# First half of the SSD output projection: ten of its eleven late units as five pairs by seven products of quarters, the residual kept in DRAM, weight buffers of half the size

## The chip, the cores and the metric

The kernel runs on one core of a Trainium2 chip. The metric is device time in microseconds (us) of one execution. Engines are named as in the profile: PE (TensorE, matmuls), PEld (its weight loads), DVE (VectorE), ACT (ScalarE), POOL (GpSimd) and SP (SyncE, which issues most DMAs).

## The reference

Two layers over 512 tokens of width 2048: a Mamba-2 SSD mixer, then a stick-breaking attention mixer; each is followed by a gate from the residual. The change lies in the first layer's output projection, `y @ out_w` with K = 4096, and in its residual.

```python
def reference(x, p, norm_w, ssd_in_w, ...):
    h = x
    for i in range(DEPTH):
        u = rms_norm(h, norm_w[i])
        if i % N_MIXERS == 0:
            mix = ssd_branch(u, ...)      # ends in  y @ out_w,  y (512, 4096), out_w (4096, 2048)
        else:
            mix = sb_branch(u, ...)       # ends in  o @ out_w,  o (512, 2048)
        h = h + mix
        gate = sigmoid(rms_norm(h, ple_norm_w[i]) @ ple_gate_w[i])
        h = h + (p[i] @ ple_proj_w[i]) * gate
    return h
```

## The kernel before

Everything is laid out transposed: a tile has 128 features (partitions) by T = 512 tokens. An fp32 operand is split into a high and a low part, `ah`, `al` for activations and `wh`, `wl` for weights, and each product is three matmuls (h x h, h x l, l x h). The high part is a cast on ACT, the low part a subtraction on DVE (`split`, L144/L145; `block`, L135 load, L137 cast, L139 subtraction).

A `unit` makes one output tile of 128 features: K/128 k-tiles, three matmuls of 512 columns each, in one PSUM bank (`mmp`, tag "mm", four banks). A `pair` makes two output tiles at once, and for 8 of its 16 k-tiles it may use the seven-product scheme (Strassen, in Winograd's form) on 2 x 2 quarters: two output tiles by two k-tiles for the weights, two k-tiles by two halves of 256 tokens for the activations. The sums of weight quarters come from `wforms` (S1 to S4, one call per four k-tiles, b = 0 and 1), the sums of activation halves from `xforms` (`th`, `tl`, from a raw tile U and a scratch US; SP = 4 of them cover 8 k-tiles). Its seven products go to four banks Z, W, X, Y, each product three matmuls of 256 columns for g = 0 and g = 1, so 84 matmuls for both b; the other eight k-tiles are `plain`, 24 matmuls of 512 for each of the two output tiles. Afterwards ACT and DVE combine the banks (L279 to L283, then L291 for each output tile) in a tile E, and `emit` takes the result. With `late` the plain products come first.

The output projection of the SSD layer has K = 4096, 32 k-tiles of `y`, which stands in DRAM (`y_d`). Its first half, k-tiles 0 to 15, is done by 16 units: five (j < EARLY) at the end of the scan, with the residual x added and the sum written to `h_d` (L666 to L671), and eleven afterwards (L777 to L779), added to `h[j]` in SBUF; the 16 tiles `h[j]` are loaded by SP (L774). The second half is eight pairs with `forms` (L781 to L784), whose eight k-tiles are 16 to 23; `staged2` loads its 16 k-tiles as eight tiles U through POOL's queue (two buffers, L707) and splits them. Each pair's `emit` is `add_h` (L722).

The attention layer's output projection (`w_sp`, `w_sq`) uses the same `pair` and `wforms`; there several pairs have no plain products. PE's instructions run in program order. The other engines' orders come from a scheduler; what stands in `high_priority` (the weights, in `block` and `wforms`) is put ahead of the rest. Each engine works its queue in order, and a DMA queue's issues wait in order too.

## Time and profile before

| what | value |
|---|---|
| median of 3 runs | 2732.29 us (2732.17 to 2732.33) |
| the profiled execution's own time | 2730.93 us |
| its span | 2729.0 us |
| PE busy | 2718.0 us, 13242 matmuls |
| DVE, ACT, POOL busy | 1654.1, 1299.9, 379.9 us |
| DMA | 304.81 MB, mean 112 GB/s |

The span runs from the first to the last instruction of the profiled execution; its own time is 1.93 us more. An engine's busy time is what its instructions took; idle time of an engine that nobody waits for costs nothing. PE's waits say where the others came late.

### The profile page before, as it was taken

What the parts mean: (1) busy time and instruction counts of PE and PEld (TensorE: products, weight loads), DVE (VectorE), ACT (ScalarE), POOL (GpSimd) and SP (SyncE); (2) the same over time, 40 slices, a digit from 0 to 9 for tenths busy, and PEclk for the clock granted to TensorE, in tenths of its full rate; (3) what the DMA queues carried; (4) which work ended last, traced back from release to release, by engine and by line L of the source; (5) the groups of instructions that cost most, each with busy time, mean ns of one, the idle gap of its engine ahead of it and who ended that gap; (6) DMA issues with size and microseconds to landing.
All of it is one profiled execution on the core that took longest, in us unless ns stands there. A gap on an engine that the chain in (4) does not pass through costs nothing.

```text
span 2729.0 us, 34056 instructions
## 1 busy us (share of the span) xinstructions
PE 2718.0 (100%) x13242; PEld 2267.4 (83%) x13242; DVE 1654.1 (61%) x2203; ACT 1299.9 (48%) x2014; POOL 379.9 (14%) x406
## 2 busy tenths in 40 slices
PE   9999999999999999999999999999999999999999
PEld 7888888888888888889888888888888888889887
DVE  8665566565565675376744547647647647779533
ACT  6554545546464553243432436646546546544321
POOL 2222121222222121011110100000000000112000
PEclk9999999999999999999999999999999999999999
DMA  4343323334243447243333322322222222343342
GB/s 170 114 128 99 124 93 124 101 116 128 94 135 94 142 143 247 93 143 105 101 101 94 100 93 93 93 89 87 88 97 85 87 91 88 106 158 105 112 124 85
DMA packets 110257, 304.81 MB, mean 112 GB/s; under 512 B 11472, under 2 KB 27472, under 8 KB 110096
## 3 DMA queue, kind: packets, MB, share of 16 engines
q1 hardware_dynamic: 106576, 291.10, 33.7%
q0 software_dynamic: 3520, 11.54, 1.3%
q8 instruction: 104, 1.70, 0.3%
q14 instruction: 57, 0.47, 0.1%
HBM read 284.37 MB, written 18.22 MB: 111 GB/s over the span
## 4 chain that ended last, share of the span: by engine, by line
PE 95%; DVE 2%; DMA 1%; ACT 1%; issue 1%; POOL 0%; SPq 0%; DVEq 0%; POOLq 0%; ACTq 0%
PE mm L57 79%; PE pv L57 6%; PE px_p L57 2%; PE px_r L57 1%; PE px_y L57 1%; PE px_z L57 1%; PE px_av L57 1%; PE px_o L57 1%; PE px_st L57 1%; PE px_qn L57 1%; PE px_x L60 1%; DMA raw<-in_w_op 0%; DVE al L145 0%; PE psB L57 0%; PE psd L57 0%
## 5 line engine op out<-in xcount | busy, mean ns | idle before, releaser
L57 PE MATMUL mm<-ah,wh 128*128 128x512 f32 (+1 forms) x3252 | 1257.9, 387 | 0.6 <-ACT ah L144 0.6
L57 PE MATMUL mm<-ah,wl 128*128 128x512 f32 (+1 forms) x3252 | 1249.5, 384 | 0.1
L57 PE MATMUL mm<-al,wh 128*128 128x512 f32 (+1 forms) x3252 | 1247.3, 384 | 1.5 <-DVE al L145 1.5
L139 DVE TENSOR_TENSOR wl<-raw,wh 128x1024 fp32r<-128x1024 f32 x424 | 529.7, 1249 | 413.3 <-ACT wh L137 412.2
L137 ACT CAST wh<-raw 128x1024 fp32r<-128x1024 f32 x424 | 444.6, 1049 | 646.7 <-PE mm L57 528.0
L57 PEld LDWEIGHTS mm<-ah,wl 128*128 128x128 f32 x3252 | 611.1, 188 | 123.4 <-DVE wl L139 0.4
L57 PEld LDWEIGHTS mm<-al,wh 128*128 128x128 f32 x3252 | 611.7, 188 | 121.1 <-DVE al L145 3.1
L57 PEld LDWEIGHTS mm<-ah,wh 128*128 128x128 f32 x3252 | 611.5, 188 | 116.9 <-issue 0.9
L685 POOL TENSOR_TENSOR ssq<-ssq,sq 128x512 f32<-128x512 f32 x45 | 68.0, 1512 | 407.3 <-ACT sq L684 407.3
L879 POOL TENSOR_SCALAR_AFFINE_SELECT lm<-lm 128x128 f32<-128x128 f32 x64 | 27.8, 434 | 614.9 <-DVE lm L878 612.1
L520 DVE SCALAR_TENSOR_TENSOR cv<-xr,vec,cv 128x512 f32<-128x512 f32 x144 | 109.7, 762 | 2.8
L57 PE MATMUL pv<-wh,ah 128*128 128x512 f32 x256 | 101.0, 395 | 0.0
L57 PE MATMUL pv<-wl,ah 128*128 128x512 f32 x256 | 99.9, 390 | 0.0
L57 PE MATMUL pv<-wh,al 128*128 128x512 f32 x256 | 99.7, 389 | 0.0
L592 ACT ACTIVATE M<-ab,act__458 128x128 f32<-128x128 f32 x256 | 84.0, 390 | 30.3 <-PE px_y L57 29.9
L210 ACT CAST wh<-raw 128x768 fp32r<-128x768 f32 (+1 forms) x60 | 54.6, 941 | 80.5 <-DVE raw L204 49.2
L313 ACT ACTIVATE sg<-cv 128x512 f32<-128x512 f32 x48 | 30.3, 632 | 125.7 <-DVE cv L520 125.6
L756 DVE TENSOR_TENSOR gt<-mm,rbc 128x512 f32<-128x512 f32 x32 | 22.1, 691 | 101.9 <-PE mm L57 101.8
L315 POOL TENSOR_TENSOR xc<-cv,sg 128x512 f32<-128x512 f32 x32 | 42.2, 1318 | 254.9 <-ACT sg L314 234.9
L876 DVE SCALAR_TENSOR_TENSOR lb<-px_z,e 128x128 f32<-128x128 f32 (+1 forms) x64 | 31.4, 490 | 72.6 <-ACT e L874 72.1
L211 DVE TENSOR_TENSOR wl<-raw,wh 128x768 fp32r<-128x768 f32 (+1 forms) x60 | 65.5, 1094 | 8.9 <-ACT wh L210 8.9
L57 PE MATMUL mm<-th,wh 128*128 128x256 f32 x240 | 68.0, 283 | 0.7 <-DVE h L779 0.7
(252 smaller groups left out, 3126.1 us busy)
## 6 DMA issues: line engine op xcount, KB each, us to landing
raw<-in_w_in SPq DMA_DIRECT2D x158, 512.0 KB, 3.5
raw<-in_w_sb SPq DMA_DIRECT2D x96, 512.0 KB, 3.5
raw<-in_w_gate SPq DMA_DIRECT2D x64, 512.0 KB, 3.9
ab<-ac_d SPq DMA_DIRECT2D x64, 256.0 KB, 3.4
raw<-in_w_oe SPq DMA_DIRECT2D x32, 512.0 KB, 3.6
raw<-in_w_op SPq DMA_DIRECT2D x32, 512.0 KB, 4.1
raw<-in_w_v SPq DMA_DIRECT2D x32, 512.0 KB, 3.6
y_d<-zs SPq DMA_DIRECT2D x32, 256.0 KB, 3.8
```

Source lines behind the costliest of these rows:

```text
L57: self._queue(self.tc.nc.tensor.matmul(out, lhsT, rhs, start=start, stop=stop, **kw), rows / 2370.0)
L137: S.copy(wh, raw)
L139: V.tensor_tensor(wl, raw, wh.bitcast(F32), op=ALU.subtract)
L210: S.copy(wh, raw)
L211: V.tensor_tensor(wl, raw, wh.bitcast(F32), op=ALU.subtract)
L313: S.activation(tmp, half, AF.Tanh)
L315: G.tensor_tensor(dst, half, tmp, op=ALU.mult)
L520: V.scalar_tensor_tensor(cv, xr[:, tap : tap + T], cw[:, u, tap : tap + 1], cv, op0=ALU.mult, op1=ALU.add)
L592: S.activation(M[:, c, :], ab[:, c * P : (c + 1) * P], AF.Relu, bias=act_[:, c, h : h + 1], scale=-1.0)
L685: G.tensor_tensor(ssq, ssq, sq, op=ALU.add)
L876: V.scalar_tensor_tensor(lb, pz, 0.0, e, op0=ALU.min, op1=ALU.subtract)
L879: G.affine_select(out=lm[:, :P], in_=lm[:, :P], compare_op=ALU.is_gt, fill=0.0, base=0, pattern=[[1, P]], channel_multiplier=-1,)
```

## The change

The unit j = 5 stays a unit; the ten units j = 6 to 15 become five pairs with seven products for k-tiles 0 to 7 (`first`: four forms, kept in the slots h0 to h7 of the residual's pool) and plain products for k-tiles 8 to 15; the first pair is `late`. The residual of these tiles no longer stands in SBUF: `set_down` loads x into one buffer hx, adds, and writes the sum to `h_d`, all DMAs on POOL's queue, and after the last pair 16 loads on POOL's queue bring the residual back as eight tiles hp. The second half's forms are made from the middle of the pairs on (j = 10). In `wforms` the quarters are loaded as they are, in 8 k-tiles of 128 columns, three of them split directly (768 columns), and S3, S1, S2, S4 made by four DVE operations of 256 columns in a tile Q of one buffer, then split (1024 columns). In `pair` the order of the seven products is A11, A12, A22, S3, S1, S2, S4 instead of A11, S3, S1, S2, A12, S4, A22, and E shares the tag and the two buffers of U. The raw weights have four buffers of 8 tiles (512 KB) instead of two of 16. The line numbers move by one or so: L697 to L707 becomes L706 for the U loads, L291 becomes L290, L281/L282/L283 become L280/L281/L282.

```diff
@@ -131,7 +131,7 @@
 
     def block(src, offset=4000):
         with tc.high_priority(offset=offset):
-            raw = wp.tile([P, 16, P], F32, tag="raw", name="raw", bufs=2)[:, :8, :]
+            raw = wp.tile([P, 8, P], F32, tag="raw", name="raw", bufs=4)
             nc.sync.dma_start(raw, src)
             wh = wp.tile([P, 8, P], F32R, tag="wh", name="wh")
             S.copy(wh, raw)
@@ -190,36 +190,35 @@
 
 
 
-
         with tc.high_priority(offset=4000):
-            F = wp.tile([P, 8, 2, P], F32, tag="raw", name="raw", bufs=2)
-            nc.sync.dma_start(F.rearrange("p (a b) g m -> p a b (g m)", b=2)[:, :, 0, :], src)
-            V.tensor_tensor(F[:, 1], F[:, 0], F[:, 2], op=ALU.subtract)
-            V.tensor_tensor(
-                F[:, 2:6].rearrange("p (a b) g m -> p a b (g m)", b=2)[:, :, 1, :],
-                F[:, 4].rearrange("p g m -> p (g m)").unsqueeze(1).broadcast_to([P, 2, 2 * P]),
-                F[:, 0:2].rearrange("p a g m -> p a (g m)"),
-                op=ALU.add,
-            )
-            V.tensor_tensor(F[:, 7], F[:, 6], F[:, 5], op=ALU.subtract)
-            out = []
-            for tag, a, b, pool in (("", 1, 5, wp), ("3", 5, 8, wq)):
-                wh = pool.tile([P, 2 * (b - a), P], F32R, tag="wh" + tag, name="wh")
-                wl = pool.tile([P, 2 * (b - a), P], F32R, tag="wl" + tag, name="wl")
-                raw = F[:, a:b].rearrange("p a g m -> p (a g) m")
-                S.copy(wh, raw)
-                V.tensor_tensor(wl, raw, wh.bitcast(F32), op=ALU.subtract)
-                out += [(wh, wl, 2 * i) for i in range(b - a)]
-        return out
-
-    def xforms(raw, i):
+            R = wp.tile([P, 8, P], F32, tag="raw", name="raw", bufs=4)
+            nc.sync.dma_start(R, src)
+            A21, A11, A22, A12 = (R[:, 2 * i : 2 * i + 2, :] for i in range(4))
+            Q = wq.tile([P, 8, P], F32, tag="Q", name="Q", bufs=1)
+            S3, S1, S2, S4 = (Q[:, 2 * i : 2 * i + 2, :] for i in range(4))
+            wh = wq.tile([P, 6, P], F32R, tag="wh3", name="wh")
+            wl = wq.tile([P, 6, P], F32R, tag="wl3", name="wl")
+            S.copy(wh, R[:, 2:8, :])
+            V.tensor_tensor(S3, A21, A11, op=ALU.subtract)
+            V.tensor_tensor(S1, A22, A21, op=ALU.add)
+            V.tensor_tensor(S2, A22, S3, op=ALU.add)
+            V.tensor_tensor(S4, A12, S2, op=ALU.subtract)
+            V.tensor_tensor(wl, R[:, 2:8, :], wh.bitcast(F32), op=ALU.subtract)
+            vh = wp.tile([P, 8, P], F32R, tag="wh", name="wh")
+            vl = wp.tile([P, 8, P], F32R, tag="wl", name="wl")
+            S.copy(vh, Q)
+            V.tensor_tensor(vl, Q, vh.bitcast(F32), op=ALU.subtract)
+        return [(wh, wl, 2 * i) for i in range(3)] + [(vh, vl, 2 * i) for i in range(4)]
+
+    def xforms(raw, i, slots=None):
 
         t = tp.tile([P, 4, H], F32, tag="US", name="US")
         V.tensor_tensor(t[:, 0:2], raw[:, 0:1].broadcast_to([P, 2, H]), raw[:, 1:3], op=ALU.subtract)
         V.tensor_tensor(t[:, 2], raw[:, 2], t[:, 0], op=ALU.subtract)
         V.tensor_tensor(t[:, 3], raw[:, 3], t[:, 2], op=ALU.subtract)
-        th = tp.tile([P, 4, H], F32R, tag=f"th{i}", name=f"th{i}")
-        tl = tp.tile([P, 4, H], F32R, tag=f"tl{i}", name=f"tl{i}")
+        pool, tags = slots or (tp, (f"th{i}", f"tl{i}"))
+        th = pool.tile([P, 4, H], F32R, tag=tags[0], name=f"th{i}")
+        tl = pool.tile([P, 4, H], F32R, tag=tags[1], name=f"tl{i}")
         split(th, tl, t)
         return th, tl
 
@@ -257,7 +256,7 @@
             plain(0, X)
             plain(1, Y)
         for b in range(len(forms) // 2):
-            S3, A11, S1, A22, S2, A12, S4 = wforms(src[:, b, :].rearrange("p (a n) -> p a n", a=4))
+            A11, A22, A12, S3, S1, S2, S4 = wforms(src[:, b, :].rearrange("p (a b) -> p a b", b=P))
             for m in range(7):
                 for g in range(2):
                     i = 2 * b + g
@@ -266,16 +265,16 @@
                     lo, hi = slice(0, H), slice(H, T)
                     seven(*(
                         (Z, 1, A11, g, ah[:, hi], al[:, hi]),
+                        (X, 1, A12, g, bh[:, hi], bl[:, hi]),
+                        (Y, 1, A22, g, th[:, 3], tl[:, 3]),
                         (W, 1, S3, g, th[:, 1], tl[:, 1]),
                         (W, 0, S1, g, th[:, 0], tl[:, 0]),
                         (Z, 0, S2, g, th[:, 2], tl[:, 2]),
-                        (X, 1, A12, g, bh[:, hi], bl[:, hi]),
                         (X, 0, S4, g, bh[:, lo], bl[:, lo]),
-                        (Y, 1, A22, g, th[:, 3], tl[:, 3]),
                     )[m])
                 fl.poll()
         if forms:
-            E = tp.tile([P, 4, H], F32, tag="E", name="E")
+            E = tp.tile([P, 4, H], F32, tag="U", name="E", bufs=2)
             S.copy(E[:, 1], Z[:, 1])
             U2 = tp.tile([P, T], F32, tag="gt", name="U2")[:, :H]
             V.tensor_tensor(U2, Z[:, 0], E[:, 1], op=ALU.add)
@@ -769,14 +768,31 @@
         wq = st.enter_context(tc.tile_pool(name="wq0", bufs=2, reuse_waits="tile"))
         tp = st.enter_context(tc.tile_pool(name="tp0", bufs=1, reuse_waits="tile"))
         lq = st.enter_context(tc.tile_pool(name="lq0", bufs=1, reuse_waits="tile"))
-        for j in range(KT):
-            h.append(lp.tile([P, T], F32, tag=f"h{j}", name=f"h{j}"))
-            nc.sync.dma_start(h[j], (h_d if j < EARLY else xT)[j * P : (j + 1) * P, :])
+
+        def set_down(j0):
+            def emit(o, e):
+                js = slice((j0 + o) * P, (j0 + o + 1) * P)
+                hx = lq.tile([P, T], F32, tag="sq2", name="hx")
+                G.dma_start(hx, xT[js, :])
+                V.tensor_tensor(hx, e, hx, op=ALU.add)
+                G.dma_start(h_d[js, :], hx)
+            return emit
+
+
+        first = [
+            xforms(quarters(from_dram(y_d), 2 * i), i, (lp, (f"h{2 * i}", f"h{2 * i + 1}"))) for i in range(SP)
+        ]
+        set_down(EARLY)(0, unit(w_oe[EARLY], acts))
+        for j in range(EARLY + 1, KT, 2):
+            if j == EARLY + 5:
+                forms = forms_of(from_dram(y_d), KT)
+            pair(w_of[(j - EARLY) // 2], acts, first, 0, set_down(j), late=j == EARLY + 1)
         ssq = rp.tile([P, T], F32, tag="ssq", name="ssq")
-        forms = forms_of(from_dram(y_d), KT)
-        for j in range(EARLY, KT):
-            ps = unit(w_oe[j], acts)
-            V.tensor_tensor(h[j], ps, h[j], op=ALU.add)
+        for j in range(0, KT, 2):
+            hp = lp.tile([P, 2, T], F32, tag=f"h{j // 2}", name="hp")
+            for q in range(2):
+                h.append(hp[:, q, :])
+                G.dma_start(h[j + q], h_d[(j + q) * P : (j + q + 1) * P, :])
         acts = staged2(y_d, KT, 2 * KT)
         for j in range(0, KT, 2):
             if j == KT - 2:
```

The weights of j = 6 to 15 are laid out as pairs on the host (`w_of`), and `h_d` has all 16 tiles.

**POOL, entry into the second half.** Before, from the last of the second half's forms on (a row with x2 is the two loads of one tile; U_8674 is that form's tile, U_9367 to U_9433 are the activations):

```order
L707 DMA U_8674<-y_d_75 128x512 x2
L707 DMA U_9367<-y_d_75 128x512 x2
L707 DMA U_9378<-y_d_75 128x512 x2
L707 DMA U_9389<-y_d_75 128x512 x2
L707 DMA U_9400<-y_d_75 128x512 x2
L707 DMA U_9411<-y_d_75 128x512 x2
L707 DMA U_9422<-y_d_75 128x512 x2
L707 DMA U_9433<-y_d_75 128x512 x2
```

Now, from the loads behind the last pair of the first half on (hx_9692 and hx_9727 are that pair's residual tiles, U_9756 is the first tile of the second half's activations):

```order
L795 DMA hp_9744<-h_d_78 128x512 x2
L795 DMA hp_9747<-h_d_78 128x512 x2
L795 DMA hp_9750<-h_d_78 128x512 x2
L706 DMA U_9756<-y_d_75 128x512 x2
L778 DMA h_d_78<-hx_9692 128x512
L776 DMA hx_9727<-in_xT 128x512
L795 DMA hp_9753<-h_d_78 128x512
L706 DMA U_9767<-y_d_75 128x512 x2
L778 DMA h_d_78<-hx_9727 128x512
L706 DMA U_9778<-y_d_75 128x512 x2
L795 DMA hp_9753<-h_d_78 128x512
L706 DMA U_9789<-y_d_75 128x512 x2
```

The U loads of the second half stood directly behind one another, and now have loads and writes of the residual before and between them.

**DVE, first pair of the first half, its second group of products (b = 1).** Before, where eleven units ran on PE meanwhile, the last two of the four forms were made so (US, then tl; wl is a weight block, h an add of a unit):

```order
L218 TENSOR_TENSOR US_8666<-U_8663 128x512
L139 TENSOR_TENSOR wl_8844<-raw_8840,wh_8842 128x1024
L219 TENSOR_TENSOR US_8666<-U_8663,US_8666 128x256
L220 TENSOR_TENSOR US_8666<-U_8663,US_8666 128x256
L145 TENSOR_TENSOR tl2_8671<-US_8666,th2_8670 128x1024
L218 TENSOR_TENSOR US_8677<-U_8674 128x512
L779 TENSOR_TENSOR h6_8620<-mm_8747,h6_8620 128x512
L139 TENSOR_TENSOR wl_8876<-raw_8872,wh_8874 128x1024
L219 TENSOR_TENSOR US_8677<-U_8674,US_8677 128x256
L220 TENSOR_TENSOR US_8677<-U_8674,US_8677 128x256
L145 TENSOR_TENSOR tl3_8682<-US_8677,th3_8681 128x1024
```

Now the last form's rows (US_8644, tl3_8649) stand so among weight forms of the next pair (Q_8917, Q_8974) and splits (wl):

```order
L210 TENSOR_TENSOR wl_8927<-Q_8917,wh_8926 128x1024
L145 TENSOR_TENSOR tl2_8638<-US_8633,th2_8637 128x1024
L206 TENSOR_TENSOR wl_8919<-raw_8915,wh_8918 128x768
L202 TENSOR_TENSOR Q_8974<-raw_8972 128x256
L203 TENSOR_TENSOR Q_8974<-raw_8972 128x256
L204 TENSOR_TENSOR Q_8974<-raw_8972,Q_8974 128x256
L216 TENSOR_TENSOR US_8644<-U_8641 128x512
L205 TENSOR_TENSOR Q_8974<-raw_8972,Q_8974 128x256
L217 TENSOR_TENSOR US_8644<-U_8641,US_8644 128x256
L218 TENSOR_TENSOR US_8644<-U_8641,US_8644 128x256
L210 TENSOR_TENSOR wl_8984<-Q_8974,wh_8983 128x1024
L145 TENSOR_TENSOR tl3_8649<-US_8644,th3_8648 128x1024
```

Between tl2 and tl3 one weight split stood; now there are two (wl_8919, wl_8984) and four operations Q.

**DVE, from the first pair to the second.** At the end of a pair the banks are read by L281, L282, L283 and L291 before, here after the first pair of the second half:

```order
L282 TENSOR_TENSOR E_9569<-mm_9456,U2_9571 128x2x256
L204 TENSOR_TENSOR raw_9702<-raw_9702 128x256
L283 TENSOR_TENSOR E_9569<-mm_9456,E_9569 128x256
L145 TENSOR_TENSOR pl_10784<-U_10785,ph_10783 128x1024
L211 TENSOR_TENSOR wl_9712<-raw_9702,wh_9711 128x768
L211 TENSOR_TENSOR wl_9708<-raw_9702,wh_9707 128x1024
L291 TENSOR_TENSOR E_9569<-mm_9457,E_9569 128x512
L722 TENSOR_TENSOR h0_8608<-E_9569,h0_8608 128x512
L291 TENSOR_TENSOR E_9569<-mm_9458,E_9569 128x512
```

Now, after the first pair of the first half (mm_8717 to mm_8720 are its banks Z, W, X, Y, wl_9039 is a block of the next pair's plain products):

```order
L206 TENSOR_TENSOR wl_8976<-raw_8972,wh_8975 128x768
L280 TENSOR_TENSOR U2_8897<-mm_8717,E_8895 128x256
L281 TENSOR_TENSOR E_8895<-mm_8718,U2_8897 128x2x256
L282 TENSOR_TENSOR E_8895<-mm_8718,E_8895 128x256
L139 TENSOR_TENSOR wl_9039<-raw_9035,wh_9037 128x1024
L290 TENSOR_TENSOR E_8895<-mm_8719,E_8895 128x512
L290 TENSOR_TENSOR E_8895<-mm_8720,E_8895 128x512
L777 TENSOR_TENSOR hx_8902<-E_8895,hx_8902 128x512
```

Before, three splits stood among the reads of a pair whose plain products were still running; now a block's split stands between L282 and the first L290, after a pair whose plain products came first.

## Rows read from the trace of the kernel before

**Rows 1.** The page: busy time of each engine; shares of the chain that ended last.

```profile
PE 2718.0 (100%) x13242; PEld 2267.4 (83%) x13242; DVE 1654.1 (61%) x2203; ACT 1299.9 (48%) x2014; POOL 379.9 (14%) x406
...
PE 95%; DVE 2%; DMA 1%; ACT 1%; issue 1%; POOL 0%; SPq 0%; DVEq 0%; POOLq 0%; ACTq 0%
```

**Rows 2.** Waits of PE, 1050 to 1340 us: who waited for whom, total, times, longest.

```profile
PE mm L57 <- DVE al L145: 0.8, 2, 0.4
PE mm L57 <- DVE h L779: 0.7, 1, 0.7
```

**Rows 3.** Timeline of PE, 1059 to 1329 us: start, duration, instruction.

```profile
1059.44 0.39 PE L57 MATMUL mm<-ah,wh 128*128 128x512 f32 x1
...
1179.12 0.28 PE L57 MATMUL mm<-ah,wh 128*128 128x256 f32 x1
...
1202.49 0.28 PE L57 MATMUL mm<-ah,wh 128*128 128x256 f32 x1
...
1212.56 0.40 PE L57 MATMUL mm<-ah,wh 128*128 128x512 f32 x1
...
1328.37 0.28 PE L57 MATMUL mm<-ah,wh 128*128 128x256 f32 x1
```

**Rows 4.** Groups by form, 1050 to 1340 us, DVE and ACT: count, busy, mean ns, idle before.

```profile
L139 DVE TENSOR_TENSOR wl<-raw,wh 128x1024 fp32r<-128x1024 f32 x38 | 46.4, 1222 | 36.1 <-ACT wh L137 36.0
...
L211 DVE TENSOR_TENSOR wl<-raw,wh 128x768 fp32r<-128x768 f32 x16 | 15.3, 954 | 6.3 <-ACT wh L210 6.3
...
L145 DVE TENSOR_TENSOR al<-U,ah 128x512 fp32r<-128x512 f32 x16 | 10.6, 689 | 4.7 <-ACT ah L144 4.7
...
L204 DVE TENSOR_TENSOR raw<-raw 128x256 f32<-128x256 f32 x16 | 6.8, 424 | 0.4
...
L137 ACT CAST wh<-raw 128x1024 fp32r<-128x1024 f32 x38 | 39.9, 1050 | 92.4 <-PE mm L57 90.7 <-DMA raw<-in_w_op 1.6
...
L210 ACT CAST wh<-raw 128x768 fp32r<-128x768 f32 x16 | 13.4, 835 | 44.7 <-DVE raw L204 44.7
...
L144 ACT CAST ah<-U 128x512 fp32r<-128x512 f32 x16 | 9.8, 619 | 10.3 <-DMA U<-y_d 10.1
```

**Rows 5.** Timeline of POOL, 1174 to 1190 us: issues of U loads, three of six.

```profile
1174.51 1.07 POOL L707 DMA_DIRECT2D U<-y_d  x2 [88.09 <-DVE al L145]
1176.81 1.07 POOL L707 DMA_DIRECT2D U<-y_d  x2 [1.23 <-DVE al L145]
...
1189.47 1.07 POOL L707 DMA_DIRECT2D U<-y_d  x2 [1.42 <-DMA raw<-in_w_op]
```

**Rows 6.** DMA issues: operation, count, KB each, median us from issue to landing.

```profile
U<-y_d POOLq DMA_DIRECT2D x24, 256.0 KB, 4.1
...
hx<-in_xT SPq DMA_DIRECT2D x5, 256.0 KB, 2.6
h_d<-hx SPq DMA_DIRECT2D x5, 256.0 KB, 2.0
```

**Rows 7.** Windows, attention projection: length, busy PE, PEld, DVE, ACT, POOL, clock, DMA.

```profile
2453.00:2483.00 30.00, 30.00 (x252) 30.00 (x252) 29.46 (x44) 13.52 (x20) 8.12 (x5) 1.00 0.33 99
```

**Rows 8.** Timeline of DVE there: the first and last of five U2 operations.

```profile
2441.63 0.42 DVE L281 TENSOR_TENSOR U<-mm,E 128x256 f32<-128x256 f32 x1
...
2492.20 0.41 DVE L281 TENSOR_TENSOR U<-mm,E 128x256 f32<-128x256 f32 x1
```

**Rows 9.** Waits there, of PE (2380 to 2545 us) and DVE (2430 to 2520).

```profile
PE mm L57 <- DVE wl L211: 0.2, 1, 0.2
...
DVE raw L197 <- DMA raw<-in_w_sp: 4.6, 3, 2.7
```

**Rows 10.** Timeline of PE at the start: the first of six and the next.

```profile
5.04 0.77 PE L57 MATMUL psd<-ah,wh 128*64 128x512 f32 x1
...
7.58 0.39 PE L57 MATMUL psd<-ah,wh 128*64 128x512 f32 x1
```

**Rows 11.** Windows at the start, columns as above.

```profile
5.00:7.40 2.40, 2.40 (x8) 1.64 (x8) 1.78 (x5) 1.69 (x4) 0.00 (x0) 1.00 0.99 310
```

More of the change, by code (lines that the diff above doesn't have):

```diff
@@ L86, in trunk @@
 def trunk(
-    ctx: ExitStack, tc: tile.TileContext, xT, pT, vecs, hvecs, consts, w_dt, w_in, w_oe, w_op, w_sb, w_v, w_se, w_sp, w_sq, w_gate, w_ple, out
+    ctx: ExitStack, tc: tile.TileContext, xT, pT, vecs, hvecs, consts, w_dt, w_in, w_oe, w_of, w_op, w_sb, w_v, w_se, w_sp, w_sq, w_gate, w_ple, out
 ):
@@ L103, in trunk @@
     ac_d = dram.tile([NH, T], F32, name="ac_d")
-    h_d = dram.tile([EARLY * P, T], F32, name="h_d")
+    h_d = dram.tile([D, T], F32, name="h_d")
     def px(name="px"):
@@ L356, in __init__ @@
                 if raws is None:
-                    raw = wp.tile([P, 16, P], F32, tag="raw", name="raw", bufs=2)
+                    raw = wp.tile([P, 8, P], F32, tag="raw", name="raw", bufs=4)
                     raws = raw[:, 0:4, :], raw[:, 4:8, :]
@@ L1042, in _layout @@
         "hvecs": np.stack([i["ssd_dt_bias"][0], i["ssd_a_log"][0]], axis=1), "consts": consts,
-        "w_dt": w_dt, "w_in": _units(in_w, order), "w_oe": _units(ow[:D], slice(None)),
+        "w_dt": w_dt, "w_in": _units(in_w, order), "w_oe": _units(ow[:D], slice(0, (EARLY + 1) * P)), "w_of": _pairs(ow[:D, (EARLY + 1) * P :], 0),
         "w_op": _pairs(ow[D:], 0),
```

## The prediction

> **What bounds the kernel now.** I read the page first: TensorE is busy for 2718.0 of 2729.0 us, and the chain that ended last is 95% PE [rows 1]. So a change can win only by taking matmul columns away, and it loses whatever it makes PE wait. The second view is PE's waits around the place of the change, 1050 to 1340 us: three, of 1.5 us together [rows 2]. The third is PE's timeline there. Eleven units with K = 16 run from 1059.44 to 1179.12, so a unit takes 119.68/11 = 10.88 us, 0.2267 us for each of its 48 matmuls of 512 columns. Six pairs of the second half, with seven products each, run from 1202.49 to 1328.37, 125.88/6 = 20.98 us a pair; the first of them spends 10.07 us on 84 matmuls of 256 columns (0.12 each) and 10.91 on 48 of 512 [rows 3]. The profiled execution took 2730.93 us, its span plus 1.93; the median of the runs is 1.36 more, which I add at the end. About 0.2% (5.5 us) is what a measurement of this kernel can tell from no change.
>
> **1. Products.** Ten of the eleven units become five pairs of the form already measured: 20.98 us where two units cost 21.76. 5 x 0.78 = **-3.9 us**, all on the path.
>
> **2. The old entry into the second half.** Its first pair ran from 1179.12 to 1202.49, 23.37 us instead of 20.98: it waited 0.69 us for VectorE's h add and twice for a late al [rows 2, 3]. Part 5 takes the place of all this: **-2.3**.
>
> **3. The first pair of the first half.** The forms th, tl were made while the eleven units ran; now pair 0 wants them. Its plain products come first (it is `late`): unit j=5 from 1059.4, then 10.9 of plain products, so the seven products start at about 1081.2; call that t = 0. PE wants tl3 after 58 matmuls of 256 (42 of the first half, then A11, A12 and four of A22, third in the new order): t = 6.96. What stands ahead of tl3 is in the order rows of VectorE above. The chain starts with the cast wh_8918, whose buffer PE frees after 18 matmuls, t = 2.16. From there by [rows 4]: that cast (768 columns) 0.83, its wl 0.95, three Q operations at 0.42, the 512 of US_8644 0.69, the fourth Q 0.42, then on ScalarE the casts wh_8983 and th3 at 1.05 each, and tl3 1.22. That ends at t = 9.6, which is 2.7 late by bare durations; for the hand-overs between engines I take 0.3: **+3.0**. Bounds: 0 (the scheduler's rows run closer together than their durations, as VectorE's do where they don't depend on each other), and 4.5 (0.2 us for each of nine hand-overs).
>
> **4. From pair 0 to pair 1.** No plain products lie between their seven products, and both use the same four PSUM banks. The new order wants X and Y second and third, no longer fifth and seventh, and pair 1's Y gets the bank of pair 0's X, which L290 reads. In VectorE's order a weight split, wl_9039, stands ahead of L290; it waits for its cast, and that for pair 0's last product. From that product: cast 1.05, wl 1.22, L290 0.69 [rows 4], 2.96 us, against 12 matmuls of 256 (1.44) that PE still has: 1.5, with hand-overs **+1.7**. Bounds 0 (the split done earlier) and 3 (no cover at all). Between the later pairs 10.9 us of plain products cover this, the hx adds and the four forms of the second half (VectorE 0.69 + 2 x 0.42 + 1.22 each): **0**, at most 1.5. Without that cover the hx chain (write 2.0, load 2.6 [rows 6], one buffer) would show.
>
> **5. The new entry into the second half** is the largest term. Before, six U loads were issued by GpSimd from 1174.51 to 1189.47, 2.99 us apart, each as an al freed one of two buffers. GpSimd had waited 88 us for the first, and it came 4.6 us ahead of the second half's first pair [rows 5]; by then two tiles were loaded. Now hp loads, h_d writes and hx loads stand on GpSimd's queue before U_9756 and between it and U_9767. Count from the end of the last pair's seven products; the second half should begin at 10.9, after two plain parts. Six hp loads wait for slots that those products read: 3.2 us of issue at 0.54. U_9756 follows, and lands at about 8 (4.1 to land). Two casts of 0.62 and two splits of 0.69 [rows 4, 6] end between 10 and 11.5, since wl_9917 and Q operations stand ahead of al1. U_9767 reuses that buffer, and so is issued between 10.4 and 11.8. The lower end is also what GpSimd's own queue gives: L290 and the hx add end at 6.9, the write lands 2.3 later, hx and hp are issued after it. I take 11.8, because al1 stands in a VectorE queue with eight other operations. Six more tiles share two buffers: 6 x 2.99 = 17.9; issue and landing 4.6, split 1.3, so al15 is there at 35.6. PE has 27 matmuls of 512 (6.1 us) from its first use on, and ends at 41.7 where 10.9 + 21.0 = 31.9 was wanted; some of this runs closer, I take **+9.5**. Bounds: 5 (U_9767 at 10.4, tiles 2.3 apart, as the first two of [rows 5]) and 13 (3.5 apart).
>
> GpSimd's own speed is no term: it issued two U loads in 1.07 us in each of [rows 5], beside a VectorE at work. The Trainium skill, "DMA: Bandwidth & Descriptors", section "SWDGE vs HWDGE vs iDMA", speaks against moving these transfers from SP to GpSimd: GpSimd writes descriptors into SBUF, from which VectorE can lock it out. By that rule, were each of the six hp issues ahead of U_9756 held for one operation of 0.69, the sum would be 4 us higher; the trace disagrees so far, with its 1.07 for two.
>
> **6. The attention output projection** has pairs without plain products, where VectorE bounds nearly as much as PE: busy 29.5 of 30 us in 2453 to 2483, and five U2 operations (L281) from 2441.63 to 2492.20, 12.6 us apart, where PE needs 84 x 0.12 = 10.1 [rows 7, 8]. PE lived on what VectorE had done ahead, until one wait of 0.2 us [rows 9]. The new `wforms` has four operations of 256 (4 x 0.42) for 0.42 + 0.69 + 0.42: 0.15 more, twice a pair, 1.5 us over five pairs. It also needs the split of the raw quarters before the first product, 0.8 more: **+2.3**. Bounds: -0.7 (VectorE's waits for raw, 4.6 us in three [rows 9], shrink with four buffers) and +6 (0.3 per form more, from rows that depend on each other).
>
> The rest (half-size weight buffers under plain units, the gates, the scan) is covered by PE: it waits for no weight elsewhere, so a weight that comes earlier brings **0**.
>
> **Sum:** -3.9 - 2.3 + 3.0 + 1.7 + 9.5 + 2.3 = +10.3; 2730.93 + 10.3 + 1.36 = 2742.6, given as **2742.5 us**.
>
> **Rivals.**
> A. *The U loads come in time* (the other side). If al15 were there 9.5 us earlier, PE would not wait in part 5. That is decided by U_9767: issued at 2 instead of 11.8, or tiles 1.4 us apart instead of 2.99. Then the sum is +0.8: 2733.1, within 0.2%; with half of part 5 hidden, 2738. For it: VectorE is idle 39% of the span. Against it: the order of GpSimd's queue, and the closest tiles of [rows 5] are 2.3 apart.
> B. *All new waits are hidden* by what PE has ahead. -6.2 gives 2726.1, faster by just over 0.2%; 3 us of remaining waits give 2729. For it: PE waited only 1.5 us here. Against it: at each of the three places the order shows the late operation behind others.
> C. *A slow restart after the new wait.* At the start of the program, behind the short warm-up matmuls, six of 512 took 2.54 us, 0.42 apart, not 0.2267, with a granted clock of 1.00, the 2.4 GHz level [rows 10, 11]. If part 5's wait, of some 5 us at its longest, did this to the last 27 matmuls of that pair, they would cost 27 x 0.2 = 5.3 more: 2748. Against it: the whole of [rows 2]'s stalls cost 2.39 us by part 2, 0.9 more than the waits themselves. The Trainium skill, "TensorE: Matmul & The Clock Gate", Part 1, says that the gate halves the clock when the array has been idle; no row here shows a granted clock under 1.00.
> D. *The attention pairs are VectorE's*: part 6 at +6, or part 5 at its upper bound: 2746 to 2752.
>
> **How the numbers follow.** Forecast 0.58, from 2737 to 2748; A 0.17; B 0.08, half of it under 2726.8; C 0.06; D 0.11. Faster: 0.04. Within 0.2% (2726.8 to 2737.8): B's other half, most of A and the forecast's lower edge, 0.20. Slower 0.76. The range 2733 to 2751 leaves out B, a part of A below its middle and the tail of D.
>
> **What would show it.** Right: five pairs in the first half whose plain and seven parts take 21 us; a wait of PE for tl3 or th3 of 2 to 4 us in the first; a shorter one for L290 behind it; U_9767 issued after the second half's start, and its first pair some 9 us over 20.98; a wait for wl near the end of the attention pairs, longer than 0.2. Wrong: a second half that starts with waits under 1 us; then A holds, and part 5 is the step that failed.

## The result: 2760.7 us, slower by about 1%

| | before | changed |
|---|---|---|
| median | 2732.31 us (4 runs, 2732.17 to 2735.19) | 2760.72 us (4 runs, 2759.30 to 2765.05) |
| ratio | | 1.0105, 95% interval 1.0093 to 1.0118 |
| profiled execution: own time, span | 2730.93, 2729.0 us | 2759.30, 2757.5 us |
| PE matmuls | 13242 | 13422 |

The forecast was 2742.5 with a range from 2733 to 2751; the time lies above it. The sign was right, the size not.

The page after (busy times; below them the shares of the chain that ended last), beside [rows 1]:

```profile
PE 2723.7 (99%) x13422; PEld 2278.6 (83%) x13422; DVE 1717.5 (62%) x2324; ACT 1312.9 (48%) x2033; POOL 405.0 (15%) x452
...
PE 90%; DVE 3%; issue 2%; DMA 2%; ACT 1%; POOL 1%; SPq 0%; DVEq 0%; POOLq 0%; ACTq 0%
```

PE's share of the chain fell by five points; DVE, DMA, POOL and issue gained one each, by rounded shares. Where this happened, PE's waits in 1050 to 1340 us say (who waited for whom, total, times, longest); [rows 2] had two lines there:

```profile
PE mm L57 <- ACT ah L144: 11.6, 3, 6.7
PE mm L57 <- DVE E L282: 3.7, 2, 3.4
PE mm L57 <- ACT th L144: 2.1, 1, 2.1
PE mm L57 <- DVE al L145: 1.2, 3, 0.6
PE mm L57 <- DVE U L280: 1.1, 2, 0.9
PE mm L57 <- DVE tl L145: 1.1, 1, 1.1
PE mm L57 <- DVE E L290: 0.8, 1, 0.8
```

Those are 21.6 us of waits, where before there were 1.5. PE's timeline after answers to [rows 3]: the first matmul of each pair's seven products in the first half, the first of the second half (1193.61) and of its second pair (1228.52), and some that waited:

```profile
1081.66 0.28 PE L57 MATMUL mm<-ah,wh 128*128 128x256 f32 x1
...
1097.29 0.39 PE L57 MATMUL mm<-ah,wh 128*128 128x256 f32 x1 [0.21 <-DVE U L280]
...
1119.91 0.28 PE L57 MATMUL mm<-ah,wh 128*128 128x256 f32 x1
...
1142.12 0.39 PE L57 MATMUL mm<-ah,wh 128*128 128x256 f32 x1 [0.91 <-DVE U L280]
...
1146.55 0.36 PE L57 MATMUL mm<-ah,wh 128*128 128x256 f32 x1 [3.45 <-DVE E L282]
...
1168.38 0.28 PE L57 MATMUL mm<-ah,wh 128*128 128x256 f32 x1
...
1193.61 0.39 PE L57 MATMUL mm<-ah,wh 128*128 128x256 f32 x1 [4.09 <-ACT ah L144]
...
1201.56 0.58 PE L57 MATMUL mm<-ah,wh 128*128 128x256 f32 x1 [6.70 <-ACT ah L144]
...
1204.45 0.41 PE L57 MATMUL mm<-th,wh 128*128 128x256 f32 x1
1204.66 0.41 PE L57 MATMUL mm<-tl,wh 128*128 128x256 f32 x1
...
1228.52 0.28 PE L57 MATMUL mm<-ah,wh 128*128 128x256 f32 x1
```

Against 10.07 us for seven products and 20.98 for a pair [rows 3], each stretch has its loss. First pair's products: 15.63 - 10.07 = 5.6 (and they began 0.5 late). Second pair: 22.62 - 20.98 = 1.6. Third: 1.2. Fourth: 26.26 - 20.98 = 5.3. The fifth and the first pair of the second half took 1228.52 - 1168.38 = 60.14, less 41.96: 18.2, all behind the entry at 1168.38 + 20.98 = 1189.36. So the second half's second pair began at 1228.52 where it had begun at 1202.49: 26.0 us of the 28.5 by which the span grew. The attention projection gave 1.7 more; 0.8 stands elsewhere.

| part of the prediction | forecast | measured |
|---|---|---|
| 1 products saved | -3.9 | -3.9 |
| 2 old entry | -2.3 | -2.4 |
| 3 first pair | +3.0 | +6.0 |
| 4 first to second pair; later pairs | +1.7; 0 | +1.6; +6.5 |
| 5 new entry | +9.5 (5 to 13) | +18.2 |
| 6 attention projection | +2.3 | +1.7 |
| rest | 0 | +0.8 |
| sum | +10.3 | +28.5 |

### The profile page after: what moved, and what is told of

The parts are those of the page before. It is cut to its first block, busy times and chain, and to the rows that moved or that the text cites. A ratio compares the mean times of both kernels' runs of the same rounds, so it can differ in the third digit from the quotient of the medians.

```text
span 2757.5 us, 34703 instructions
## 1 busy us (share of the span) xinstructions
PE 2723.7 (99%) x13422; PEld 2278.6 (83%) x13422; DVE 1717.5 (62%) x2324; ACT 1312.9 (48%) x2033; POOL 405.0 (15%) x452
## 4 chain that ended last, share of the span: by engine, by line
PE 90%; DVE 3%; issue 2%; DMA 2%; ACT 1%; POOL 1%; SPq 0%; DVEq 0%; POOLq 0%; ACTq 0%
PE mm L57 74%; PE pv L57 6%; PE px_p L57 1%; PE px_r L57 1%; PE px_y L57 1%; PE px_z L57 1%; PE px_av L57 1%; PE px_o L57 1%; DMA h_d<-hx 1%; PE px_st L57 1%; DMA U<-y_d 1%; PE px_qn L57 1%; PE px_x L60 1%; DVE al L145 0%; DVE wl L206 0%
## 5 line engine op out<-in xcount | busy, mean ns | idle before, releaser
L57 PE MATMUL mm<-ah,wl 128*128 128x512 f32 (+1 forms) x3232 | 1236.6, 383 | 1.0 <-DVE wl L206 1.0
L57 PE MATMUL mm<-al,wh 128*128 128x512 f32 (+1 forms) x3232 | 1234.9, 382 | 2.5 <-DVE al L145 2.2
L139 DVE TENSOR_TENSOR wl<-raw,wh 128x1024 fp32r<-128x1024 f32 x414 | 518.5, 1253 | 399.2 <-ACT wh L137 397.0
L137 ACT CAST wh<-raw 128x1024 fp32r<-128x1024 f32 x414 | 433.5, 1047 | 604.0 <-PE mm L57 500.0
L57 PE MATMUL mm<-th,wh 128*128 128x256 f32 x320 | 93.1, 291 | 3.4 <-ACT th L144 2.1
L57 PE MATMUL mm<-tl,wh 128*128 128x256 f32 x320 | 92.8, 290 | 1.1 <-DVE tl L145 1.1
L57 PE MATMUL mm<-th,wl 128*128 128x256 f32 x320 | 92.6, 289 | 0.0
L209 ACT CAST wh<-Q 128x1024 fp32r<-128x1024 f32 x40 | 42.0, 1049 | 81.2 <-PE mm L57 47.1
```

The source lines that it names most:

```text
L57: self._queue(self.tc.nc.tensor.matmul(out, lhsT, rhs, start=start, stop=stop, **kw), rows / 2370.0)
L137: S.copy(wh, raw)
L139: V.tensor_tensor(wl, raw, wh.bitcast(F32), op=ALU.subtract)
L209: S.copy(vh, Q)
```

## The entry and the fourth pair in the trace

GpSimd's timeline of the changed kernel (issues of DMAs; 1178.45 is the end of the last pair's seven products):

```profile
1177.94 0.54 POOL L776 DMA_DIRECT2D hx<-in_xT  x1 [2.90 <-DMA h_d<-hx]
1178.47 3.27 POOL L795 DMA_DIRECT2D hp<-h_d  x6
1182.32 1.19 POOL L795 DMA_DIRECT2D hp<-h_d  x2 [0.58 <-issue]
1183.88 2.54 POOL L795 DMA_DIRECT2D hp<-h_d  x4 [0.37 <-issue]
1186.52 0.55 POOL L706 DMA_DIRECT2D U<-y_d  x1
1188.37 0.54 POOL L706 DMA_DIRECT2D U<-y_d  x1 [1.31 <-DMA hp<-h_d]
...
1194.57 0.54 POOL L776 DMA_DIRECT2D hx<-in_xT  x1 [3.99 <-DMA h_d<-hx]
...
1195.79 1.07 POOL L706 DMA_DIRECT2D U<-y_d  x2
...
1217.14 1.07 POOL L706 DMA_DIRECT2D U<-y_d  x2 [2.30 <-DVE al L145]
```

The two loads of U_9756 went out 8.1 and 9.9 us behind the products, not 3 to 4: twelve hp loads were issued from 1178.47 on and ahead of them, and the second waited for an hp load to land. Six of the twelve had stood behind the hx load of 1177.94, which waited 2.9 us for an h_d write to land. U_9767 went out at 17.3, behind an hx load that had waited 4 us for its write to land. From there to U_9833 are six distances of 3.56 us, not 2.99. Windows of the entry (length, busy PE, PEld, DVE, ACT, POOL, granted clock, DMA share, GB/s):

```profile
1175.00:1180.00 5.00, 5.00 (x38) 4.74 (x37) 3.40 (x6) 2.25 (x3) 2.04 (x5) 1.00 0.99 347
1180.00:1185.00 5.00, 5.00 (x23) 4.14 (x23) 3.44 (x7) 1.05 (x1) 3.81 (x8) 1.00 0.95 340
1185.00:1190.00 5.00, 4.52 (x20) 3.39 (x19) 2.77 (x5) 0.00 (x0) 2.23 (x5) 1.00 1.00 367
1190.00:1195.00 5.00, 0.91 (x3) 0.48 (x3) 1.41 (x3) 2.03 (x3) 0.97 (x2) 0.97 0.57 220
1195.00:1200.00 5.00, 0.00 (x0) 0.00 (x0) 2.64 (x4) 0.15 (x1) 2.96 (x7) 0.50 0.69 222
1200.00:1205.00 5.00, 3.30 (x12) 2.79 (x13) 1.39 (x2) 1.86 (x3) 1.10 (x3) 0.50 0.70 250
```

The DMA engines are full while the hp loads run (16 x 256 KB are 4.2 MB, 12 us at 350 GB/s), and PE's granted clock is at half in the last two windows. The fourth pair's wait begins on GpSimd too. Two timelines, of VectorE and of ScalarE, at the third pair's end:

```profile
1133.28 0.69 DVE L216 TENSOR_TENSOR US<-U 128x512 f32<-128x512 f32 x1 [4.49 <-DMA U<-y_d]
...
1141.65 0.42 DVE L280 TENSOR_TENSOR U<-mm,E 128x256 f32<-128x256 f32 x1
...
1142.71 1.22 DVE L210 TENSOR_TENSOR wl<-Q,wh 128x1024 fp32r<-128x1024 f32 x1
1143.84 1.22 DVE L145 TENSOR_TENSOR tl<-US,th 128x1024 fp32r<-128x1024 f32 x1
...
1145.98 0.42 DVE L282 TENSOR_TENSOR E<-mm,E 128x256 f32<-128x256 f32 x1
```

```profile
1135.68 1.05 ACT L144 CAST th<-US 128x1024 fp32r<-128x1024 f32 x1 [7.50 <-DVE US L218]
...
1137.58 0.36 ACT L278 COPY E<-mm 128x256 f32<-128x256 f32 x1
```

VectorE sat 4.5 us before a form whose U load had stood on GpSimd behind an h_d write, and with it ScalarE, whose copy into E stands behind that form's cast. The third pair's seven products had ended at 1130.1; U2 read its bank at 1141.65 and L282 at 1145.98, behind splits and forms, and the fourth pair waited for these banks.

## The experiments

Three theories stood: **Q**, the order of GpSimd's queue; **E**, E in U's two buffers; **B**, the crowd of hp loads on the DMA engines. Later came **R**, the round trip of the single hx buffer, and the PSUM **banks**. Each run is told by its median, its ratio to the kernel before with its interval, and by two losses read from PE's timeline as above: in the five pairs (entry against 1059.44 + 10.88 + 5 x 20.98 = 1175.22) and at the entry (the first two pairs of the second half against 41.96). The changed kernel has 14.1 and 18.2.

**Residual on SP's queue** (e_sp).

```diff
-                G.dma_start(hx, xT[js, :])
+                nc.sync.dma_start(hx, xT[js, :])
...
-                G.dma_start(h_d[js, :], hx)
+                nc.sync.dma_start(h_d[js, :], hx)
...
-                G.dma_start(h[j + q], h_d[(j + q) * P : (j + q + 1) * P, :])
+                nc.sync.dma_start(h[j + q], h_d[(j + q) * P : (j + q + 1) * P, :])
```

> The residual's three kinds of DMA (hx load, h_d write, hp load) go from GpSimd's queue to SP's; nothing else changes. Theory Q (order of GpSimd's queue: U loads stand behind residual DMAs that wait for adds and landings): the entry into the second half loses 9 us or less instead of 18, and the 6 us at the start of the fourth pair go, so 2738 to 2746. Theory E (E shares the two U buffers): the fourth pair still waits, 2755 to 2760. Theory B (the 16 hp loads fill the DMA engines, so U lands late whatever the queue): 2757 to 2762.

2753.57 us, 1.0079 (1.0062 to 1.0096); losses 12.7 and 13.1. Q has a part, 5 us of the entry, but not the fourth pair: the wait for E L282 there is 3.45 us as before. The first U load now goes out at 1171.25, 5.8 us ahead of the end of the last pair's products, although an hp load took longer to land (median 6.5 us, 5.2 on GpSimd's queue). No theory gave this time; more than one cause is at work.

**hp loads written behind the activations** (e_ufirst): the loop over hp moves below `acts = staged2(...)`.

> The hp loads are written behind the activations of the second half, so some U loads stand ahead of hp loads on GpSimd's queue; hx and h_d stay between them. Theory Q: the entry into the second half loses 5 to 9 us less, the fourth pair's wait stays: 2751 to 2756. Theory E: within 2 us of the changed kernel, 2758 to 2762. Theory B: the U loads come before the crowd and gain as under Q, but the hp loads then share the engines with the later U loads: 2754 to 2759.

2760.41 us, 1.0102 (1.0087 to 1.0117), losses 19.3 and 16.4: no gain, which is what E forecast. U_9767's counterpart did go out earlier, 10.6 us behind the products instead of 17.3, but the six distances behind it grew to 4.19 us, with hx and h_d transfers still between them, and the five pairs lost 5.2 us more. So this run proves little for or against Q.

**E in a buffer of its own** (e_etag), paid for by three raw buffers instead of four.

```diff
-            E = tp.tile([P, 4, H], F32, tag="U", name="E", bufs=2)
+            E = tp.tile([P, 4, H], F32, tag="E", name="E")
```

> E gets a buffer of its own again (three raw weight buffers instead of four pay for it). Theory E: the fourth pair's 6 us go, and U_9778 need not wait for the last hx add, 2 to 4 us at the entry: 2750 to 2754. Theory Q: VectorE still sits 4.5 us before a US operation whose U load stood behind an h_d write, and the copy into E stands behind that form's cast on ScalarE, so the fourth pair still loses 3 to 6 us and the entry all of its 18: 2757 to 2762.

2755.26 us, 1.0083 (1.0068 to 1.0098), losses 11.9 and 15.0; the time lies between the two forecasts. The fourth pair starts 21.07 us after the third and loses nothing, as E says; the second pair's wait grew (PE for U2 L280, 3.7 us). Waits of PE, 1050 to 1340 us:

```profile
PE mm L57 <- DVE E L290: 4.4, 1, 4.4
PE mm L57 <- DVE U L280: 3.7, 1, 3.7
PE mm L57 <- ACT ah L144: 2.2, 2, 1.7
...
```

The entry now waits for a bank (E L290) and less for ah, since more U loads are out early: two of its eight tiles U went out before 1122, where the changed kernel's first went out at 1186.52.

**Both** (e_sp_etag).

> Both edits: residual's DMAs on SP's queue, E in a buffer of its own (three raw buffers). Alone they gave 2753.6 and 2755.3 (7.1 and 5.4 below the changed kernel). If queue and shared buffer are separate causes: the sum, 2747 to 2749. If together they free the entry (each U load then waits only for its own al): 2741 to 2745. Theory B (16 hp loads crowd the DMA engines, shown at a share near 1.0 from 1175 to 1205 in the run with SP): the entry keeps 8 us or more, 2747 to 2750.

2747.44 us, 1.0055 (1.0040 to 1.0070), losses 10.1 and 8.1. Alone the two gave 7.1 and 5.5, together they give 13.3 of the 28.4 us: about the sum, so Q and E are separate causes. The entry still loses 8.1, as B said, so this run does not decide about B.

**hp loads spread over the second half** (e_sp_lazy, e_sp_etag_lazy, e_sp_pace). First the loads were written ahead of each pair:

> As the run with the residual on SP, but each hp pair is loaded ahead of its own pair of the second half (two loads a pair) and not all 16 before the activations. Theory B: U loads land in 4 us again, the entry loses 4 to 8 us less: 2746 to 2750. Without B (queue order and buffers alone): within 2 us of 2753.6.

> All three: residual on SP, E in its own buffer, hp loads spread over the second half. If these three are what the entry and the fourth pair lost (18 and 6 us, less the 2.3 of before), there remain the first pair's forms and its banks, 7 to 9 us, less 3.9 for the columns, plus 1.5 for wforms: 2737 to 2742. If something else holds the entry: above 2745.

2753.94 us, 1.0077 (1.0062 to 1.0092), and 2748.18 us, 1.0058 (1.0042 to 1.0075). Neither tested B: the scheduler put the loads where they had been. SP's timeline has seven of them issued from 1176.37 on in e_sp and from 1177.07 on in e_sp_lazy. Then, on the kernel of e_sp, each load was held behind the last weight load of the pair before:

```diff
+                tc.add_manual_dep(
+                    ld.ins,
+                    last_raw[0].ins.name,
+                    mybir.DependencyInfo(mybir.DependencyClass.NoSync, mybir.DependencyReason.DATA),
+                    reason="order",
+                )
```

> As the run with the residual on SP, with the hp loads of each pair held in SP's queue behind the weight loads of the pair before (the spread that the earlier run asked for and did not get, its 16 loads went out at the same times). Theory B (the crowd): the DMA share at the entry falls from 1.0, U loads land in about 4 us, the entry loses 4 to 8 us less than with SP alone: 2746 to 2750. Without B: within 2 us of 2753.6.

2751.52 us, 1.0068 (1.0053 to 1.0083); the entry lost 10.7 instead of 13.1, the five pairs 14.2 instead of 12.7. The median is 2 us lower than e_sp's, and the intervals overlap: a gain of 4 to 8 is not seen. The crowd was thinned and not removed, with a DMA share of 0.65 to 0.98 from 1175 to 1205.

**Banks in turn** (e_banks): pairs use the banks of the two PSUM pools alternately, as the attention projection does.

> The changed kernel with its pairs taking the PSUM banks of the two pools in turn, as the attention projection does; nothing else. If the waits for U2, E L282 and E L290 are PSUM bank waits (first to second pair 2 us, fourth pair 6, with the slow matmuls behind them), they go: 2752 to 2754. The entry's waits for ah stay. If the banks are only where a late VectorE shows, PE waits for its weights instead and the time stays within 2 us of 2760.7.

2759.78 us, 1.0101 (1.0084 to 1.0117), losses 6.0 and 26.5. PE's waits, 1050 to 1340 us:

```profile
PE mm L57 <- ACT ah L144: 16.9, 3, 10.5
PE mm L57 <- ACT th L144: 2.2, 1, 2.2
PE mm L57 <- DVE al L145: 1.2, 3, 0.6
PE mm L57 <- DVE tl L145: 1.1, 1, 1.1
```

All waits for U2 and E are gone, and every microsecond comes back at the entry. So the banks did not pace the first half here. By e_sp and e_etag the chain of E, hx and U loads has a part in what did, and PE waits for it in one place or the other.

**Two hx buffers** (e_hx2), and with the banks in turn (e_hx2_banks); three raw buffers pay for it.

```diff
-                hx = lq.tile([P, T], F32, tag="sq2", name="hx")
+                hx = lq.tile([P, T], F32, tag="hx", name="hx", bufs=2)
```

> The changed kernel with two buffers for the residual tile hx instead of one (three raw buffers pay for it), all on GpSimd's queue as before. Theory R (the round trip of the single hx buffer, 7 to 10 us from one add to the next, holds the h_d writes, and behind them the hp and U loads): U_9756 goes out several us earlier, the entry loses 4 to 9 us less: 2750 to 2756. Theory Q alone (order of the queue, whatever hx's buffers): the hp loads still stand ahead, 2758 to 2762.

> Two hx buffers and the banks in turn, on the changed kernel. With the banks alone PE lost nothing in the pairs after the first, but 10.7 us more at the entry's first wait, so something else than PE paced the entry. If that was the hx round trip: pairs without waits and an entry of 14 us at most, 2745 to 2752. If it was the shared buffer of E and U, or the hp crowd: 2756 to 2760.

2761.69 us, 1.0108 (1.0094 to 1.0121), losses 17.6 and 18.4; and 2756.84 us, 1.0094 (1.0078 to 1.0109), losses 8.2 and 21.4. R alone gained nothing. With the banks in turn the second hx buffer may be worth 3 us (against e_banks), but these two intervals overlap.

**The edits of the forms alone** (e_wf): the kernel before with the new `wforms`, order of products, E in U's buffers and raw buffers, without the five pairs.

> The kernel before with the new wforms, the new order of the seven products, E in U's buffers and four half-size raw buffers, without the five pairs. If part 6 of the prediction has its size: 2734.6 (plus 2.3). By the changed kernel's trace, where the attention pairs lost about 1.4 us more than before: 2733 to 2735. If these edits cost something in the second half too (E waits for U): above 2736.

2734.18 us (10 runs), 1.0007 (0.9998 to 1.0016): 1.6 us above before, within what can be told from no change. Its attention pairs wait as those of the changed kernel do (2380 to 2545 us; L289 is L290 there), where [rows 9] had one wait of 0.2:

```profile
PE mm L57 <- DVE wl L206: 1.0, 2, 0.7
PE mm L57 <- DVE E L289: 0.5, 2, 0.2
...
```

**Units for j = 5, 6, 7 and four pairs** (best1): with the residual on SP, E alone and the hp loop of e_sp_lazy.

```diff
-        set_down(EARLY)(0, unit(w_oe[EARLY], acts))
-        for j in range(EARLY + 1, KT, 2):
+        for j in range(EARLY, EARLY + 3):
+            set_down(j)(0, unit(w_oe[j], acts))
+        for j in range(EARLY + 3, KT, 2):
...
-            pair(w_of[(j - EARLY) // 2], acts, first, 0, set_down(j), late=j == EARLY + 1)
+            pair(w_of[(j - EARLY - 3) // 2], acts, first, 0, set_down(j))
```

> As the run with all three, and units for j = 5, 6 and 7, then four pairs, none of them late: the forms are made beside 32 us of units, so the first pair's wait (5 us with its slow matmuls) and the change of pair without plain products (2 to 5 us) go; the columns saved are 4 x 0.78 = 3.1. If parts 3 and 4 of the prediction have the right place: 2729 to 2734. If the forms are late for another reason: 2736 or more.

2742.74 us, 1.0036 (1.0023 to 1.0049), 5.4 less than e_sp_etag_lazy although it saves one pair's 0.8 us less. The wait for tl3 and th3 is gone, as part 3 places it, but 2729 to 2734 did not come: three waits for E L290 remain (7.6 us), and one for an hx add (2.3).

**Banks and paced loads on that version** (best2), and each alone (best1_banks, best1_pace).

> Units for j = 5 to 7, four pairs, residual on SP with paced hp loads, E in its own buffer, banks in turn. If queue, buffer, crowd and banks were the four causes, little of them is left: -3.1 for the columns, +1.5 for wforms, entry no more than the 2.4 of before: 2729 to 2733. If U's two buffers bound the entry by themselves: 2734 to 2738.

> The version with units for j = 5 to 7 (2742.7), plus the banks in turn, hp loads not paced. The two edits together gave 12.4 us. If the waits for E L290 at its entry (4.4 and 2.6 us with slow matmuls behind) are bank waits in the first place: 2731 to 2735. If they only show a VectorE that waits for weights behind the crowd of hp loads: 2738 to 2742, with PE waiting for wl instead.

> The same version plus the paced hp loads, banks not in turn. If the crowd of hp loads is the cause (VectorE waited 2.1 us for a raw weight there): 2731 to 2735. If the banks are: 2738 to 2742, with the waits for E L290 still there.

2730.29 us (10 runs), 0.9993 (0.9984 to 1.0003); 2731.60 us (10 runs), 0.9997 (0.9987 to 1.0006); 2739.52 us (9 runs), 1.0026 (1.0016 to 1.0036). Waits of PE, 1050 to 1340 us, of best2, then of best1_pace (line numbers are higher by two than in the changed kernel):

```profile
PE mm L57 <- ACT ah L146: 0.2, 1, 0.2
PE mm L57 <- DVE al L147: 0.2, 1, 0.2
```

```profile
PE mm L57 <- DVE E L292: 6.2, 2, 4.2
PE mm L57 <- DVE hx L779: 2.3, 1, 2.3
```

The same banks that gave 0.9 us on the changed kernel, not to be told from nothing, give 11.1 here: with U loads free of the residual and of E, the banks are the last large thing that PE waits for. The paced loads give 3.2 us without the banks and 1.3 with them, in both cases with intervals that overlap. In best1_banks the crowd is whole, and PE stays busy through it (windows, columns as above); its U loads go out from 1161.59 on, 14 us ahead of the second half:

```profile
1170.00:1175.00 5.00, 5.00 (x23) 4.14 (x23) 5.00 (x10) 2.29 (x3) 1.46 (x4) 1.00 1.04 394
1175.00:1180.00 5.00, 5.00 (x39) 4.80 (x39) 3.29 (x7) 1.35 (x3) 1.24 (x3) 1.00 1.03 390
1180.00:1185.00 5.00, 5.00 (x44) 5.00 (x43) 4.02 (x7) 2.71 (x4) 0.18 (x1) 1.00 1.04 390
```

**The old order of products, and the old forms, on the best version** (best3, best4).

> As the best version so far (2730.3), with the seven products in the order that they had before: X and Y late, so the small waits for E L292 in the attention pairs (four, 1.0 us with their restarts about 1.6) go; the split of the sums is wanted earlier, which may add a wait for wl. If the order of the products is what these pairs lost: 2727 to 2729. If the four operations in place of three are: within 1 us of 2730.3.

> As the best version so far (2730.3 against 2732.2 of before), with the wforms, the order of the products and the raw buffers of the kernel before. If the rewritten wforms is what the attention pairs lost (1.9 us more restarts and waits there than before): 2728 to 2729.2, faster than before by 3.1 for the columns. If the old forms make waits of their own in the first half (their splits need three dependent operations first): 2730 to 2733.

2732.81 us (11 runs), 1.0004 (0.9995 to 1.0013), and 2735.36 us (11 runs), 1.0010 (1.0001 to 1.0019). By the medians they are 2.5 and 5.1 us slower than best2, with intervals that overlap. In best3, with A12 and A22 late, PE waited longer for wl in the attention pairs (1.60 and 1.29 us, where best2's longest was 0.7). In best4 these pairs waited less (0.9 us, against 2.6 in best2), but the entry lost 6.7 us where best2's lost 1.0, with a wait for ah of 2.3. So what the rewritten forms cost in the attention pairs, the new forms with their three small buffers give back at the entry. Best4 changes forms, order and buffers together; which of them the entry needs is not shown.

The best of all is best2, 1.9 us below before. The interval of its ratio holds 1, so it isn't shown to be faster; it shows that the loss can be taken back whole, in a version with four pairs instead of five.

## Why the prediction missed

Three terms make up the 18.2 us by which the forecast fell short: part 5's +9.5 (8.7 too small), part 4's 0 for the later pairs (6.5) and part 3's +3.0 (3.0). The first two are the steps that failed.

Part 1 held: pairs without a wait cost 20.98 us. Part 2 held. So did the first half of part 4 (1.7 forecast, 1.6 found), in part by luck: 1.0 of it stands behind L290, which the step named, and 0.5 behind L282, which it did not. Rivals A and B, under which the new waits stay hidden, did not come.

Part 3 had place and mechanism right and the size wrong, beyond its bound of 4.5. "That ends at t = 9.6, which is 2.7 late": PE waited 2.1 us for th3 and 1.1 for tl3, and each restart cost more (3.6 together). What the step left out is the clock: 16 matmuls behind it came 0.21 us apart instead of 0.12, 1.6 us. The rest of the 6.0 are 0.4 at the bank and 0.5 of a late start.

Part 4 failed where it gave the later pairs **0**, "10.9 us of plain products cover this, the hx adds and the four forms". The cover was counted in VectorE's busy time; the order decides. E has to wait for a U buffer, U's load for an h_d write on GpSimd, that for an hx add, and all this stands in VectorE's and ScalarE's queues ahead of the reads of the banks. That cost 6.5 us, 5.3 of them in the fourth pair; with E in a buffer of its own (e_etag) the fourth pair lost nothing.

Part 5 named the right mechanism and missed its size by 8.7 us, beyond its bound of 13. "Six hp loads wait for slots that those products read: 3.2 us of issue" and "lands at about 8" priced a load by issue and by the landing of a quiet queue, 4.1. Six more hp loads, held up by an hx load that waited for its write, ran ahead of those, at a DMA share near 1.0. U_9767 went out 17.3 us behind the products, where 11.8 was forecast and 10.4 to 11.8 allowed (+5.5), and six distances were 3.56 (+3.4). The 4.2 MB could have been worked out: the 16 loads of h moved as much in the kernel before. But bytes are the smaller part: leaving GpSimd's queue (e_sp) took 5.1 us off the entry's 18.2, spreading the loads (e_sp_pace) 2.4 more, of which 1.5 came back in the pairs.

Of the rivals, C came true in kind, in three places. Slow matmuls cost 1.6 us behind the first pair's wait, 1.5 behind the fourth's and 2.9 at the entry, together 6.0 of the 28.4; they are part of the losses above. The forecast had 5.3 for one place with a chance of 0.06. The granted clock is 0.50, the 1.2 GHz level, from 1195 to 1205, after 5 us in which PE had been busy for 0.91, 0.51 in 1147 to 1150.4 behind the wait of 3.45, and 0.54 in 1092.5 to 1096 behind the first pair's waits of 2.1 and 1.1 with one matmul between them. After the stalls of [rows 2], under 1 us, the clock stayed at 1.00. A wait's length alone does not tell: behind one of 2.33 us in best1 the clock was 1.00, behind one of 2.29 us in best4 it was 0.58. The Trainium skill, "TensorE: Matmul & The Clock Gate", Part 1, lets an idle array fall to half its clock; by that rule the slow restart of rival C was to be expected, and the trace agrees with its 0.50.

GpSimd's own speed was nearly no term, as predicted: six hp issues took 3.27 us, 0.545 each. The next six took 3.73, with 0.95 of idle time for which the trace names no cause. What e_sp gained by leaving GpSimd's queue fits the order of that queue, as its earlier U loads show. The Trainium skill, "DMA: Bandwidth & Descriptors", section "SWDGE vs HWDGE vs iDMA", warns that VectorE, in its 2-port mode, can lock GpSimd out of the state in SBUF to which it writes descriptors; the first six issues do not show it, beside a VectorE that was busy for 3.40 and 3.44 of 5 us; whether the 0.95 is of this kind is not shown.

Part 6 was 1.7, near its 2.3; e_wf, with these edits alone, is 1.6 us slower than the kernel before, within what can be told from no change.

What stays open: what the crowd and the hx round trip cost. By medians it is 1 to 3 and about 3 us, all from runs whose intervals overlap and in versions that were changed elsewhere too. How far the banks' 11 us in best1 need the residual on SP, E's own buffer and the two further units each was not tried apart.

## What to carry to other kernels

Before giving a step 0 because an engine has idle time, follow the queue: write down, for each tile that PE will want, what stands ahead of its load, its split and the read of its bank, and whose landing each of them waits for. A buffer shared by two kinds of tile (E and U) and a DMA queue shared by two streams (residual and activations) join waits that the busy shares show as free. Where removing a wait changes nothing (e_banks), something else paces the stretch; take causes away together and then put them back one at a time.

## What was not expected of the hardware

PE's waits of 3.45 and 6.70 us cost more than themselves: a granted clock near 0.50 for the next 16 and 26 matmuls, most of them 0.21 us apart instead of 0.12. DMA engines at a share of 1.03 to 1.04 and 390 GB/s for 15 us (best1_banks) made PE wait for nothing in these 15 us, since the U loads had begun ahead. Of the scheduler, not of the hardware: writing the hp loads later in the program left them where they were on SP's queue (e_sp_lazy); a dependency moved them (e_sp_pace).
